# Cross-covariance attention: Grams of two heads over 64 partitions with masked keys, query norms from squares, query casts on GpSimd

## The chip, the core and the metric

The kernel runs on one core of a Trainium2 chip. The metric is device time in microseconds (us) of one execution, smaller is better. The core has a matrix engine (TensorE, PE in the profile; its weight loads are PEld), a vector engine (VectorE, DVE), a scalar engine (ScalarE, ACT), a general engine (GpSimd, POOL) and a sync engine (SyncE, SP), which here only issues DMA transfers. Each engine works through its own queue in order; semaphores hold an instruction back until what it needs is there.

## The reference

Q, K and V have 8 batches, 12 heads, 512 rows and 64 columns (float32). Per head the columns of Q and K are normalised over the rows, a 64x64 matrix of their products is put through a softmax, and V is multiplied by it:

```python
Q_norm = Q / (np.linalg.norm(Q, axis=-2, keepdims=True) + 1e-10)
K_norm = K / (np.linalg.norm(K, axis=-2, keepdims=True) + 1e-10)
attn = np.einsum('bhnd,bhne->bhde', Q_norm, K_norm)
attn = np.exp(attn - np.max(attn, axis=-1, keepdims=True))
attn = attn / (np.sum(attn, axis=-1, keepdims=True) + 1e-10)
return np.einsum('bhnd,bhde->bhne', V, attn).astype(np.float32)
```

Each of the three inputs and the output is 12.58 MB, so 37.75 MB are read and 12.58 MB written.

## The kernel before

**Tiling.** The 96 heads are cut into 24 units `u` of 4 heads (`HU`), two units make a pair `s` (12 pairs), two pairs a group `w` (6 groups). In a unit each head lies on 32 partitions, 16 rows (`T`) of 64 columns on each. Q and K of a pair come into one tile `qk32` of 2 MB (pool of 3), V of half a group into `v32` of 1 MB (pool of 3). Output leaves from tiles `so` of 0.5 MB (pool of 13), two for each pair.

**Stages of a unit or pair**, by the keys that the planner uses:

- `cq` (L212): VectorE casts q and k of a unit to bf16, side by side in `qkb`.
- `gr` (L232): for each row block `t` and each head a matmul of the 32 partitions' [q k] with itself; one head's Gram matrix of 128x128 holds q·q, q·k and k·k. 64 matmuls for a unit; the last unit (`WIDE`) is loaded in another layout and takes 32 over 64 partitions.
- `sq` (L239) and `rd` (L251): VectorE multiplies the diagonal blocks with an identity and sums them, which gives the squared norms of q and k. `kq` (L166 by way of `copy`): the cross block is copied out of PSUM, mostly by ScalarE.
- `pw` (L257, L258): ScalarE takes the power -1/2 as exp(-ln/2). `rq` (L269, L270) copies the q factors to where they are used. `sc` (L262): GpSimd multiplies the cross block with the k factors.
- `lg` (L275): TensorE transposes the result into PSUM. `ex` (L281): ScalarE takes the exponential with its row sum, four instructions for a pair. `nm` (L287, L290): VectorE takes a reciprocal and makes two products, written to `ab` in bf16.
- `cv` (L170 on GpSimd, L168 on VectorE): V is cast to bf16. `vt` (L301): TensorE transposes it; `vc`: the transposes are copied out of PSUM to `vt` by ScalarE, in the last groups also by VectorE.
- `ou` (L318): TensorE multiplies V with `ab`; `oc` copies the result out of PSUM to `so` by ScalarE, for the last 8 heads' pairs also by VectorE; `st` (L206) stores it.

**Order.** Nothing is ordered by the hardware across engines except by semaphores, so the order in each queue is what the program writes. `Order.run` is a planner: each piece has a cost on each engine that may take it (in the table of `piece` calls), the pieces that it needs (`after`), pieces that it has to come behind, and a rank from the table `R`; `BIAS` adds to a cost only when an engine is chosen. The planner goes through time, each time taking the startable piece of the best rank, and the kernel is emitted in the order of the planned starts. Its costs know nothing of two engines that hinder each other. Loads and stores are pieces of an engine "DMA": nearly all of them are issued by SyncE in the planned order, with at most 8 under way (`QUEUE`); each waits for the buffer that it fills or for the data that it stores. `QK_PACE`, `V_FROM`, `V_PACE` and `ST_LAG` are the ranks of loads and stores.

Of the kernel before, what the change touches and what calls it, by code (L numbers as in the profile page):

```python
# [102 lines left out]
def kernel(  # L103
# [14 lines left out]
    WIDE = U - 1  # L118
# [13 lines left out]
    Qw = Q.rearrange("b h (p j) d -> (b h p j d)", j=J).rearrange("(u m p x) -> u p m x", m=2, p=128, x=J * D)  # L132
    Kw = K.rearrange("b h (p j) d -> (b h p j d)", j=J).rearrange("(u m p x) -> u p m x", m=2, p=128, x=J * D)

# [5 lines left out]
    NB = dict(qk=3, v=3, vb=2, qkb=2, vt=2, so=13, sm=2, ab=4)  # L140
# [4 lines left out]
    qkp = ctx.enter_context(tc.tile_pool(name="qkp", bufs=NB["qkb"]))  # L145
    vtp = ctx.enter_context(tc.tile_pool(name="vtp", bufs=NB["vt"]))
# [6 lines left out]
    ps_g = grams_only.enter_context(tc.tile_pool(name="ps_g", bufs=1, space=bass.MemoryType.PSUM))  # L153
# [8 lines left out]
    qk32, v32, vb, qkb, gram, scr, kq, n2, r8, kqs, rq, lg, ex, ab, vps, vt, po, so = ({} for _ in range(18))  # L162
# [9 lines left out]
    def load_qk(s, x, r):  # L172

        w, e = divmod(s, 2)
        if s not in qk32:
            qk32[s] = qp.tile([128, 2, 2, T, D], F32, name="qk32")
        if HELD == ("l" + "qk"[x], s, r):

            nc.vector.memset(qk32[s][0:1, x, r, 0, 0:1], 0.0)
        if (s, x) == (0, 1):  # L180
            nc.scalar.dma_start(out=qk32[s][:, x, r].rearrange("p t d -> p (t d)"), in_=Ku[w, e, :, r])
        elif 2 * s + (r or 0) >= WIDE:
            nc.sync.dma_start(out=qk32[s][:, x, r].rearrange("p (m j) d -> p m (j d)", m=2), in_=(Qw, Kw)[x][U - 1])
        elif r is None:
            nc.sync.dma_start(out=qk32[s][:, x].rearrange("p r t d -> p r (t d)"), in_=(Qu, Ku)[x][w, e])
        else:
            nc.sync.dma_start(out=qk32[s][:, x, r].rearrange("p t d -> p (t d)"), in_=(Qu, Ku)[x][w, e, :, r])
# [20 lines left out]
    def cast_qk(u, x):  # L208
        s, r = divmod(u, 2)
        if x == 0:  # L210
            qkb[u] = qkp.tile([128, T, 2 * D], BF16, name="qkb")
        nc.vector.tensor_copy(qkb[u][:, :, x * D:(x + 1) * D], qk32[s][:, x, r])  # L212
# [7 lines left out]
    def grams(u):  # L220


        s, r = divmod(u, 2)
        if r == 0:
            gram[s] = ps_g.tile([128, HU, 2, 2, 2 * D], F32, name="gram")
        for t in range(T if u < WIDE else J):
            for h in range(HU):
                if u < WIDE:
                    x = qkb[u][32 * h:32 * (h + 1), t, :]
                else:  # L230
                    x = qkb[u][64 * (h % 2):64 * (h % 2 + 1), J * (h // 2) + t, :]
                nc.tensor.matmul(gram[s][:, h, r, 0], x, x, start=(t == 0), stop=(t == (T if u < WIDE else J) - 1))  # L232

    def squares(s, n):

        if n == 0:
            scr[s] = small.tile([128, 2 * HU, D], F32, name="scr")
        half = (LO, HI)[n]
        nc.vector.scalar_tensor_tensor(  # L239
            out=scr[s][half], in0=gram[s][half, :, :, 0, half].rearrange("p h r d -> p (h r) d"), scalar=1e-20,  # L240
            in1=eye2[half, None, :].to_broadcast([D, 2 * HU, D]), op0=ALU.add, op1=ALU.mult,
        )

    def cross(eng, s):

        kq[s] = small.tile([128, 2 * HU, D], F32, name="kq")
        copy(eng, kq[s][HI], gram[s][HI, :, :, 0, LO].rearrange("p h r d -> p (h r) d"))

    def sums(s):
        n2[s] = small.tile([128, 2 * HU], F32, name="n2")  # L250
        nc.vector.tensor_reduce(out=n2[s], in_=scr[s], axis=mybir.AxisListType.X, op=ALU.add)  # L251
# [8 lines left out]
    def scale_k(eng, s):  # L260
        kqs[s] = small.tile([128, 2 * HU, D], F32, name="kqs")
        (nc.vector if eng == "DVE" else nc.gpsimd).tensor_tensor(  # L262
            out=kqs[s][HI], in0=kq[s][HI], in1=r8[s][HI, :, None].to_broadcast([D, 2 * HU, D]), op=ALU.mult,
        )

    def scales_q(s):

        rq[s] = small.tile([128, HU], F32, name="rq")
        nc.scalar.copy(rq[s][LO], r8[s][LO, 0::2])  # L269
        nc.scalar.copy(rq[s][HI], r8[s][LO, 1::2])  # L270

    def logits(s):
        l = lg[s] = ps_l.tile([128, HU, D], F32, name="lg")
        for h in range(HU):
            nc.tensor.transpose(l[:, h, :], kqs[s][HI, 2 * h:2 * h + 2].rearrange("p r d -> p (r d)"), eye2[HI])  # L275

    def exps(s):
        e = small.tile([128, HU, D], F32, name="ex")
        z = small.tile([128, HU], F32, name="esum")
        for h in range(HU):  # L280
            nc.scalar.activation(e[:, h, :], lg[s][:, h, :], AF.Exp, scale=rq[s][:, h:h + 1], accum_out=z[:, h:h + 1])  # L281
        ex[s] = (e, z)
# [45 lines left out]
    for i in range(2):  # L328
        const.tile([128, D // 4], F32, name=f"front{i}")
# [15 lines left out]

    abs_ = []
# [5 lines left out]
    def size(key):  # L352
        if key[0] == "gr" and key[1] >= WIDE:
            return 64
        return 8 if key[0] == "vt" and key[-1] is not None else {"gr": 128, "lg": 8, "vt": 16, "ou": 16}[key[0]]
# [3 lines left out]
    R = dict(cq=2.5, gr=2.471, sq=0.756, kq=1, rd=3.457, pw=3.5, sc=1, rq=1.9, lg=5, ex=1.1, nm=2.545, cv=1.165, vt=0.9, vc=1.1, ou=2, oc=0.9)  # L359
    BIAS = dict(sc=-0.6, kq=5, cv=1, vc=-0.3, oc=0.6)  # L360
    QK_PACE, V_FROM, V_PACE, ST_LAG = 0.631, 0.0377, 0.7486, 1.5133
# [4 lines left out]
    def piece(key, engines, after, behind, rank, fn, *args):  # L366
        if key[0] in ("cv", "vc", "oc", "kq", "sc"):
            plan.add(key, engines, after, behind, rank, lambda eng: fn(eng, *args))
        else:
            plan.add(key, engines, after, behind, rank, lambda eng: fn(*args))  # L370
# [12 lines left out]
    for s in range(S):  # L383
        free = [back("cq", 2 * s + r, 2 * NB["qk"], x) for r in range(2) for x in range(2)]
        for r in parts(s):
            at = QK_PACE * (2 * s + (r or 0)) / U
            for x in range(2):
                key = loaded(x, s, r)
                piece(key, {"DMA": X if r is not None else 2 * X}, free, [last], at, load_qk, s, x, r)
                last = key  # L390
    for u in range(U):
        s, r = divmod(u, 2)
        piece(("cq", u, 0), {"DVE": 0.72}, [loaded(0, s, r), back("gr", u, NB["qkb"])], [back("cq", u, 1, 1)], R["cq"] + 0.01 * u, cast_qk, u, 0)
        piece(("cq", u, 1), {"DVE": 0.72}, [loaded(1, s, r)], [("cq", u, 0)], R["cq"] + 0.01 * u, cast_qk, u, 1)
        piece(("gr", u), {"PE": 1.6}, [("cq", u, 0), ("cq", u, 1), back("kq", s, 1)], [back("gr", u, 1)], R["gr"] + 0.01 * u, grams, u)
    for s in range(S):
        SM = NB["sm"]

        piece(("sq", s, 0), {"DVE": 0.70}, [("gr", 2 * s), ("gr", 2 * s + 1), back("rd", s, SM)], [], R["sq"] + 0.01 * s, squares, s, 0)
        piece(("sq", s, 1), {"DVE": 0.70}, [("gr", 2 * s), ("gr", 2 * s + 1)], [("sq", s, 0)], R["sq"] + 0.01 * s, squares, s, 1)  # L400
        piece(("kq", s), {"ACT": 0.60, "DVE": (0.70, BIAS["kq"])}, [("sq", s, 0), ("sq", s, 1), back("sc", s, SM)], [], R["kq"] + 0.01 * s, cross, s)
        piece(("rd", s), {"DVE": 0.69}, [("sq", s, 0), ("sq", s, 1), back("pw", s, SM)], [], R["rd"] + 0.01 * s, sums, s)
        piece(("pw", s), {"ACT": 0.5}, [("rd", s), back("rq", s, SM), back("sc", s, SM)], [], R["pw"] + 0.01 * s, powers, s)
        piece(("sc", s), {"POOL": (1.04, BIAS["sc"]), "DVE": 1.2}, [("pw", s), ("kq", s), back("lg", s, SM)], [], R["sc"] + 0.01 * s, scale_k, s)
        piece(("rq", s), {"ACT": 0.45}, [("pw", s), back("ex", s, SM)], [], R["rq"] + 0.01 * s, scales_q, s)
        piece(("lg", s), {"PE": 0.6}, [("sc", s), back("ex", s, 1)], [], R["lg"] + 0.01 * s, logits, s)
        piece(("ex", s), {"ACT": 1.30}, [("lg", s), ("rq", s), back("nm", s, NB["sm"])], [], R["ex"] + 0.01 * s, exps, s)
# [6 lines left out]
    for w in range(W):  # L414
# [12 lines left out]
        for n, (q, f) in enumerate(turns(w)):  # L427
# [3 lines left out]
            else:  # L431
                wait = [("kq", S - 1)] + ([("vc", w, *turns(w)[n - 4])] if n >= 4 and turns(w)[n - 4][1] is not None else [])
            piece(("vt", w, q, f), {"PE": 0.6 if f is not None else 0.8}, [("cv", w, r, c) for r in range(2) for c in range(2)] + wait, [turned],
# [7 lines left out]
    for s in range(S):  # L441
        for x in range(4):
# [4 lines left out]
            piece(("ou", s, x), {"PE": 0.5}, [("vc", s // 2, *t) for t in turns(s // 2) if t[0] // 2 == k] + [("nm", s)] + wait, order, R["ou"] + 0.01 * s, outs, s, x)  # L447
# [50 lines left out]
```

## Time and profile before

Median of 3 runs: 128.52 us (128.44 to 128.66). The profiled execution took 128.35 us, of which the profile's span, from the first instruction to the last, is 126.5 us; 1.85 us lie around it.

| engine | busy us | share of the span | instructions |
|---|---|---|---|
| PE (weight loads beside it: 64.2) | 78.9 | 62% | 2128 |
| DVE | 90.7 | 72% | 141 |
| ACT | 72.5 | 57% | 220 |
| POOL | 37.4 | 30% | 40 |
| DMA queue of SyncE (share of 16 engines) | | 96.5% | 15050 packets |

Busy time is the union of an engine's instructions; a wait inside an instruction that has begun counts as busy. The mean duration of a group can be longer than the time that its instruction needs alone, which is how one sees that something held it. The granted TensorE clock was 0.839 of full speed in the mean.

### The profile page before, as it was taken

The numbers are of one execution on the slowest core, as the hardware profiler recorded it, in microseconds if no ns is written. First come the engines' busy times: TensorE is split into PE (matmuls) and PEld (weight loads), VectorE is DVE, ScalarE is ACT, GpSimd is POOL, SyncE is SP. The second block draws the span as 40 slices with busy tenths as digits, with TensorE's granted clock in tenths as the row PEclk, the third lists the DMA queues.
The fourth block names the chain that finished last, engine by engine and source line by source line (L and its number), as shares of the span: only waits on it lengthen the run. The fifth ranks groups of instructions, "written<-read, shape, count | busy, mean of one in ns | idle before, by whom it ended". The sixth has DMA issues, their size and how long they took to land.

```text
span 126.5 us, 4885 instructions
## 1 busy us (share of the span) xinstructions
PE 78.9 (62%) x2128; PEld 64.2 (51%) x2128; DVE 90.7 (72%) x141; ACT 72.5 (57%) x220; POOL 37.4 (30%) x40
## 2 busy tenths in 40 slices
PE   0065393895964679958583999596676858473000
PEld 0054382784843568747372788484464746352000
DVE  3344749839899499899976798999999799740000
ACT  4000441539789077695883688694758969974000
POOL 4006307300745913043064303133363270300000
PEclk9999999999599555899998559959999999855555
DMA  3999999999999999999999999999999999999993
GB/s 129 408 434 411 427 413 421 413 434 408 430 417 418 409 422 417 398 414 425 422 417 412 418 419 421 416 423 423 401 415 411 402 401 407 400 407 408 405 382 149
DMA packets 15359, 50.64 MB, mean 400 GB/s; under 512 B 1130, under 2 KB 1130, under 8 KB 13930
## 3 DMA queue, kind: packets, MB, share of 16 engines
q1 hardware_dynamic: 15050, 49.29, 96.5%
q10 hardware_dynamic: 288, 1.05, 2.1%
q8 instruction: 16, 0.26, 0.7%
q14 instruction: 5, 0.04, 0.1%
HBM read 37.75 MB, written 12.58 MB: 398 GB/s over the span
## 4 chain that ended last, share of the span: by engine, by line
DVE 34%; DMA 21%; PE 19%; ACT 10%; issue 5%; POOL 2%; SPq 0%; DVEq 0%; ACTq 0%; POOLq 0%
DMA qk<-in_Q_dram 21%; DVE qkb L212 12%; PE gram L232 12%; DVE scr L239 7%; DVE ab L290 5%; ACT so L166 4%; PE po L318 3%; DVE vb L168 3%; ACT ex L281 3%; PE vps L301 3%; DVE n L251 3%; DVE vt L168 2%; ACT vt L166 2%; DVE so L168 1%; POOL kqs L262 1%
## 5 line engine op out<-in xcount | busy, mean ns | idle before, releaser
L232 PE MATMUL gram<-qkb 32*128 32x128 bf16 (+1 forms) x1504 | 36.9, 262 | 20.3 <-DVE qkb L212 7.1
L232 PEld LDWEIGHTS <-qkb 32*128 32x128 bf16 (+1 forms) x1504 | 31.0, 117 | 24.8 <-DVE qkb L212 8.9
L212 DVE CAST qkb<-qk 128x1024 bf16<-128x1024 f32 x48 | 35.3, 758 | 8.4 <-DMA qk<-in_Q_dram 6.8
L170 POOL TENSOR_SCALAR vb<-v 128x1024 bf16<-128x1024 f32 x19 | 22.0, 1169 | 43.9 <-DMA v<-in_V_dram 39.6
L166 ACT COPY so<-po 128x512 f32<-128x512 f32 x45 | 24.8, 593 | 6.6 <-PE po L318 6.5
L166 ACT COPY vt<-vps 128x1024 bf16<-128x1024 bf16 (+1 forms) x18 | 17.8, 987 | 16.5 <-PE vps L301 16.4
L318 PE MATMUL po<-ab,vt 128*64 128x128 bf16 x384 | 20.8, 252 | 5.1 <-ACT so L166 1.7
L301 PE MATMUL vps<-identb,vb 128*128 128x128 bf16 x192 | 18.4, 247 | 6.5 <-POOL vb L170 4.3
L262 POOL TENSOR_TENSOR kqs<-kq,r 64x512 f32<-64x512 f32 x12 | 14.1, 1171 | 26.7 <-ACT r L258 14.0
L239 DVE SCALAR_TENSOR_TENSOR scr<-gram,eye 64x512 f32<-64x512 f32 x24 | 16.5, 687 | 6.0 <-PE gram L232 5.8
L318 PEld LDWEIGHTS <-vt 128*64 128x64 bf16 x384 | 15.2, 127 | 9.4 <-issue 4.8
L301 PEld LDWEIGHTS <-vb 128*128 128x128 bf16 x192 | 13.5, 110 | 10.2 <-POOL vb L170 5.5
L281 ACT ACTIVATE ex<-lg,rq 128x64 f32<-128x64 f32 x48 | 14.5, 322 | 2.5 <-PE lg L275 2.3
L166 ACT COPY kq<-gram 64x512 f32<-64x512 f32 x12 | 7.0, 581 | 13.5 <-DVE scr L239 13.3
L290 DVE TENSOR_TENSOR ab<-ex,rinv 64x256 bf16<-64x256 f32 x24 | 13.4, 556 | 0.6
L281 ACT ACTIVATION_READ_ACCUMULATOR ex<-lg,rq 128x1 f32 x48 | 10.2, 213 | 0.0
L275 PE MATMUL lg<-eye,kqs 64*128 64x64 f32 x48 | 6.4, 258 | 4.3 <-POOL kqs L262 2.6
L251 DVE TENSOR_REDUCE n<-scr 128x8 f32<-128x512 f32 x12 | 8.1, 679 | 0.1
L168 DVE COPY vt<-vps 128x1024 bf16<-128x1024 bf16 (+1 forms) x8 | 7.9, 1020 | 0.1
L168 DVE CAST vb<-v 128x1024 bf16<-128x1024 f32 x5 | 7.0, 1399 | 1.3 <-DMA v<-in_V_dram 1.3
L275 PEld LDWEIGHTS lg<-eye,kqs 64*128 64x128 f32 x48 | 4.5, 156 | 6.1 <-POOL kqs L262 3.3
L287 DVE RECIPROCAL rinv<-esum 128x4 f32<-128x4 f32 x12 | 2.1, 172 | 3.4 <-ACT ex L281 3.2
(17 smaller groups left out, 16.0 us busy)
## 6 DMA issues: line engine op xcount, KB each, us to landing
out_dram<-so SPq DMA_DIRECT2D x23, 512.0 KB, 10.2
v<-in_V_dram SPq DMA_DIRECT2D x11, 1024.0 KB, 17.1
qk<-in_Q_dram SPq DMA_DIRECT2D x8, 1024.0 KB, 17.1
qk<-in_K_dram SPq DMA_DIRECT2D x8, 1024.0 KB, 17.9
qk<-in_Q_dram SPq DMA_DIRECT2D x8, 512.0 KB, 12.2
qk<-in_K_dram SPq DMA_DIRECT2D x6, 512.0 KB, 12.5
qk<-in_K_dram ACTq DMA_DIRECT2D x2, 512.0 KB
v<-in_V_dram SPq DMA_DIRECT2D x2, 512.0 KB
```

The lines of the kernel that those rows point to most:

```text
L166: nc.scalar.copy(o, i)
L168: nc.vector.tensor_copy(o, i)
L170: nc.gpsimd.tensor_scalar(out=o, in0=i, scalar1=1.0, scalar2=0.0, op0=ALU.mult, op1=ALU.add)
L212: nc.vector.tensor_copy(qkb[u][:, :, x * D:(x + 1) * D], qk32[s][:, x, r])
L232: nc.tensor.matmul(gram[s][:, h, r, 0], x, x, start=(t == 0), stop=(t == (T if u < WIDE else J) - 1))
L239: nc.vector.scalar_tensor_tensor(out=scr[s][half], in0=gram[s][half, :, :, 0, half].rearrange("p h r d -> p (h r) d"), scalar=1e-20, in1=e ...
L251: nc.vector.tensor_reduce(out=n2[s], in_=scr[s], axis=mybir.AxisListType.X, op=ALU.add)
L262: (nc.vector if eng == "DVE" else nc.gpsimd).tensor_tensor(out=kqs[s][HI], in0=kq[s][HI], in1=r8[s][HI, :, None].to_broadcast([D, 2 * HU, ...
L281: nc.scalar.activation(e[:, h, :], lg[s][:, h, :], AF.Exp, scale=rq[s][:, h:h + 1], accum_out=z[:, h:h + 1])
L290: nc.vector.tensor_tensor(out=a[half, :, half], in0=e[half], in1=ri[half, :, None].to_broadcast([D, HU, D]), op=ALU.mult,)
L301: nc.tensor.transpose(ps[:, c, n, :], vb[w][:, J * c + j].rearrange("p r d -> p (r d)"), identb)
L318: nc.tensor.matmul(po[s, x][e * D:(e + 1) * D, j].rearrange("p r d -> p (r d)"), v, ab[s][:, h, :])
```

## The change

- **Casts.** The cast of q (`cq`, x = 0) may go to GpSimd or VectorE, with a bias of -31.74 for GpSimd; in the program that comes out all 24 are on GpSimd. All 24 casts of V are on GpSimd too (19 before). In `qkb` k now lies first and q second.
- **Masks** (`mk`, new). VectorE writes a tile `km` for each unit by two products of k with a column of `pick` (1 on the partitions of even or odd heads, 0 elsewhere).
- **Grams over 64 partitions.** For each row block two matmuls of 64 partitions instead of four of 32: weights [k of the even head, k of the odd head] with zeros, moving side [k q]. 32 matmuls for every unit. A Gram tile holds k·k and k·q of both heads one above the other; q·q is not in it. `ps_g` has two buffers instead of one.
- **Norms of q** (`q2` and `nq`, new). ScalarE squares q into bf16 (`square_q`), 24 instructions; TensorE sums the squares over partitions with a mask `heads` of 4 columns, 8 matmuls for a unit (`norms_q`). ScalarE copies the sums (`hq`), VectorE adds the two halves (two instructions in `sums`).
- **Smaller pieces.** `squares`: one instruction of 128x256 for a pair instead of two of 64x512; `cross`: 128x256 instead of 64x512, in the program all on VectorE; `scale_k`: 128x256, all on GpSimd; `rq` is gone; `lg`: two transposes instead of four.
- **Order.** New ranks, biases and costs for the planner; the four ranks of loads and stores are 0. In SyncE's queue the first V load comes behind eight units of Q and K instead of behind the first two, and four stores instead of five stand before the last load. The last unit is loaded as the others are (4 KB for each partition's row instead of 2 KB pieces). In the new program VectorE copies 16 output blocks (3 before) and 5 transposed V blocks (8 before).

```diff
-    ps_g = grams_only.enter_context(tc.tile_pool(name="ps_g", bufs=1, space=bass.MemoryType.PSUM))
+    ps_g = grams_only.enter_context(tc.tile_pool(name="ps_g", bufs=2, space=bass.MemoryType.PSUM))
...
-    def cast_qk(u, x):
+    def cast_qk(eng, u, x):
         s, r = divmod(u, 2)
         if x == 0:
-            qkb[u] = qkp.tile([128, T, 2 * D], BF16, name="qkb")
-        nc.vector.tensor_copy(qkb[u][:, :, x * D:(x + 1) * D], qk32[s][:, x, r])
+            qkb[u] = qkp.tile([128, T, 2, D], BF16, name="qkb")
+        copy(eng, qkb[u][:, :, 1 - x], qk32[s][:, x, r])
+
+    def mask_k(u):
+
+        km[u] = kmp.tile([128, T, 2, D], BF16, name="km")
+        for a in range(2):
+            nc.vector.tensor_scalar(
+                out=km[u][:, :, a], in0=qkb[u][:, :, 0], scalar1=pick[:, a:a + 1], scalar2=None, op0=ALU.mult)
+
+    def square_q(u):
+        s, r = divmod(u, 2)
+        q2[u] = q2p.tile([128, T, D], BF16, name="q2")
+        nc.scalar.activation(q2[u], qk32[s][:, 0, r], AF.Square)
...
-            gram[s] = ps_g.tile([128, HU, 2, 2, 2 * D], F32, name="gram")
-        for t in range(T if u < WIDE else J):
-            for h in range(HU):
-                if u < WIDE:
-                    x = qkb[u][32 * h:32 * (h + 1), t, :]
-                else:
-                    x = qkb[u][64 * (h % 2):64 * (h % 2 + 1), J * (h // 2) + t, :]
-                nc.tensor.matmul(gram[s][:, h, r, 0], x, x, start=(t == 0), stop=(t == (T if u < WIDE else J) - 1))
...
+            gram[s] = ps_g.tile([128, 4, 4 * D], F32, name="gram")
+        for t in range(T):
+            for g in range(2):
+                rows = slice(64 * g, 64 * (g + 1))
+                nc.tensor.matmul(
+                    gram[s][:, 2 * g + r, 0:2 * D], km[u][rows, t].rearrange("p a d -> p (a d)"), qkb[u][rows, t].rearrange("p x d -> p (x d)"),
+                    start=(t == 0), stop=(t == T - 1))
+
+    def norms_q(u):
+
+        s, r = divmod(u, 2)
+        for t in range(J):
+            nc.tensor.matmul(
+                gram[s][:, 0, 2 * D + HU * r:2 * D + HU * (r + 1)], q2[u][:, 2 * t:2 * t + 2].rearrange("p t d -> p (t d)"), heads,
+                start=(t == 0), stop=(t == J - 1))
+
+    def squares(s):
+
+        scr[s] = small.tile([128, 4, D], F32, name="scr")
         nc.vector.scalar_tensor_tensor(
...
+            out=scr[s], in0=gram[s][:, :, 0:D], scalar=1e-20,
+            in1=eye2[:, None, :].to_broadcast([128, 4, D]), op0=ALU.add, op1=ALU.mult,
         )
...
-        nc.vector.tensor_reduce(out=n2[s], in_=scr[s], axis=mybir.AxisListType.X, op=ALU.add)
+        nc.vector.tensor_reduce(out=n2[s][:, 0:HU], in_=scr[s], axis=mybir.AxisListType.X, op=ALU.add)
+        for r, (here, there) in enumerate(((LO, HI), (HI, LO))):
+            cols, psum = slice(HU * r, HU * (r + 1)), slice(2 * D + HU * r, 2 * D + HU * (r + 1))
+            nc.vector.scalar_tensor_tensor(
+                out=n2[s][here, HU:2 * HU], in0=gram[s][here, 0, psum], scalar=1e-20, in1=hq[s][there, cols],
+                op0=ALU.add, op1=ALU.add)
...
-    R = dict(cq=2.5, gr=2.471, sq=0.756, kq=1, rd=3.457, pw=3.5, sc=1, rq=1.9, lg=5, ex=1.1, nm=2.545, cv=1.165, vt=0.9, vc=1.1, ou=2, oc=0.9)
-    BIAS = dict(sc=-0.6, kq=5, cv=1, vc=-0.3, oc=0.6)
-    QK_PACE, V_FROM, V_PACE, ST_LAG = 0.631, 0.0377, 0.7486, 1.5133
+    R = dict(cq=1.785, mk=3.054, q2=5.826, gr=4.546, nq=0.886, hq=0.101, sq=0.231, kq=3.274, rd=0.775, pw=0.025, sc=3.251, lg=2.932, ex=-0.237, nm=1.282, cv=1.112, vt=-5.794, vc=3.411, ou=-0.099, oc=0.151)
+    BIAS = dict(cq=-31.74, sc=-60.20, kq=-22.98, cv=64.77, vc=-0.03, oc=0.04)
+    QK_PACE, V_FROM, V_PACE, ST_LAG = 0.0000, 0.0000, 0.0000, 0.0000
...
-        piece(("cq", u, 0), {"DVE": 0.72}, [loaded(0, s, r), back("gr", u, NB["qkb"])], [back("cq", u, 1, 1)], R["cq"] + 0.01 * u, cast_qk, u, 0)
+        piece(("cq", u, 0), {"DVE": 0.72, "POOL": (1.15, BIAS["cq"])}, [loaded(0, s, r), back("gr", u, NB["qkb"])], [back("mk", u, 1)], R["cq"] + 0.01 * u, cast_qk, u, 0)
+        piece(("q2", u), {"ACT": 0.95}, [loaded(0, s, r), back("nq", u, NB["q2"])], [back("q2", u, 1)], R["q2"] + 0.01 * u, square_q, u)
         piece(("cq", u, 1), {"DVE": 0.72}, [loaded(1, s, r)], [("cq", u, 0)], R["cq"] + 0.01 * u, cast_qk, u, 1)
-        piece(("gr", u), {"PE": 1.6}, [("cq", u, 0), ("cq", u, 1), back("kq", s, 1)], [back("gr", u, 1)], R["gr"] + 0.01 * u, grams, u)
+        piece(("mk", u), {"DVE": 0.70}, [("cq", u, 1), back("gr", u, NB["km"])], [("cq", u, 1)], R["mk"] + 0.01 * u, mask_k, u)
+        piece(("gr", u), {"PE": 1.4}, [("mk", u), back("sq", s, 2), back("kq", s, 2), back("rd", s, 2)], [back("gr", u, 1)], R["gr"] + 0.01 * u, grams, u)
+        piece(("nq", u), {"PE": 0.35}, [("q2", u)], [("gr", u), back("nq", u, 1)], R["nq"] + 0.01 * u, norms_q, u)
```

## The prediction

> **What bounds the kernel now.** I read the page's totals and slices first, then the issuing queue's waits, then the end of the timeline, and last the groups and the timeline of VectorE and GpSimd. Totals and slices:
>
> ```profile
> span 126.5 us, 4885 instructions
> PE 78.9 (62%) x2128; PEld 64.2 (51%) x2128; DVE 90.7 (72%) x141; ACT 72.5 (57%) x220; POOL 37.4 (30%) x40
> DVE  3344749839899499899976798999999799740000
> DMA  3999999999999999999999999999999999999993
> SPq L206 <- DMA out_dram<-so: 10.1, 14, 1.0
> ```
>
> The DMA engines are full from the second slice (3.2 us) to the last, at about 410 GB/s: the transfers set the time. The last line, from the waits of SyncE's queue, says that 14 stores waited 10.1 us for earlier transfers, not for data. But VectorE is a close second: between 46 and 112 us its digits are 9 but for a few. So no part of the change can win much, and the question is whether the engines still finish inside the transfers' time. The end of the timeline (start us, us, what) and two 2 us windows show the margin (the last two columns are DMA share and GB/s):
>
> ```profile
> 111.41 0.85 DVE L290 TENSOR_TENSOR ab<-ex,rinv 64x256 bf16<-64x256 f32 x2
> 114.52 1.07 ACT L166 COPY so<-po 128x512 f32<-128x512 f32 x2 [0.24 <-PE po L318]
> 115.81 4.22 SPq L206 DMA_DIRECT2D out_dram<-so  x4
> 122.00:124.00 2.00, 0.00 (x0) 0.00 (x0) 0.00 (x0) 0.00 (x0) 0.00 (x0) 0.50 0.88 342
> 124.00:126.00 2.00, 0.00 (x0) 0.00 (x0) 0.00 (x0) 0.00 (x0) 0.00 (x0) 0.50 0.34 132
> ```
>
> VectorE's last work ends at 112.3, the last output copy 3.3 us later at 115.6, the transfers at 124.7 (0.34 of 2 us after 124), the span at 126.5, 1.8 us later. A store of 0.5 MB needs 1.3 us at 405 GB/s, and a transfer takes 1.4 us from issue to motion (the first load is issued at 0.74 and the engines move from about 2.1 on). So the last copy could end at 124.7 - 1.3 - 1.4 = 122.0 without moving the end: a margin of 6.4 us. Past it each us on VectorE is a us on the kernel.
>
> What can eat it is in these rows: groups (mean ns after the comma), then VectorE's and GpSimd's timelines at 39 us.
>
> ```profile
> L212 DVE CAST qkb<-qk 128x1024 bf16<-128x1024 f32 x48 | 35.3, 758 | 8.4 <-DMA qk<-in_Q_dram 6.8
> L170 POOL TENSOR_SCALAR vb<-v 128x1024 bf16<-128x1024 f32 x19 | 22.0, 1169 | 43.9 <-DMA v<-in_V_dram 39.6
> L168 DVE CAST vb<-v 128x1024 bf16<-128x1024 f32 x5 | 7.0, 1399 | 1.3 <-DMA v<-in_V_dram 1.3
> L212 DVE CAST qkb<-qk x48: 673/693/1536, 5.3 to 99.1; 128x1024 bf16<-128x1024 f32 x48
> L170 POOL TENSOR_SCALAR vb<-v x19: 1042/1048/1541, 10.7 to 101.7; 128x1024 bf16<-128x1024 f32 x19
> 39.17 2.14 DVE L212 CAST qkb<-qk 128x1024 bf16<-128x1024 f32 x2
> 39.23 1.54 POOL L170 TENSOR_SCALAR vb<-v 128x1024 bf16<-128x1024 f32 x1 [3.07 <-DMA v<-in_V_dram]
> ```
>
> A cast takes 0.69 us on VectorE and 1.05 on GpSimd (medians of the fourth and fifth line). Where both run they exclude each other: GpSimd's begins at 39.23 beside VectorE's first cast and takes 1.54, that is 0.5 waiting and 1.04 of work; it ends at 40.77. VectorE's two casts take 2.14 instead of 1.29 and end at 41.31: the second waited until GpSimd had ended. The casts of V on VectorE, made while GpSimd casts too, take 1.40 in the mean. Ops out of PSUM show no such loss (a squares pair takes 1.39 beside GpSimd and without it). The products of L290 do: 0.425 each in a pair of 0.85, 0.556 in the mean.
>
> **The change on VectorE, alone.** Removed: 24 q casts, 24 x 0.69 = -16.6; 5 casts of V, 5 x 0.69 = -3.5. Squares: two of 64x512 at 0.687 become one of 128x256. A reciprocal of 4 elements takes 0.172 and 512 elements 0.687, so 1.01 ns an element, and 256 take 0.43: 12 x 0.43 - 16.5 = -11.3. The cross copy comes from ScalarE: 12 x 0.43 = +5.2. Sums: 12 x (0.43 + two small ones at 0.17) - 8.1 = +1.1. Output copies 3 to 16: 13 x 0.69 = +9.0. V copies: four of 1.22 and one of 0.68 for 8.1 before: -2.5. Masks: 48 products of 128x1024, bf16 to bf16 in SBUF, of which the trace has none. Below, 0.17 (the reciprocal, next to no data); above, 0.69 (as many elements out of float32). The cast is the nearest row, but half of what it reads is spared, so I take the middle, 0.43: +20.6 (8.2 to 33.1). Sum: +2.0. The durations of one engine's instructions add up to 94.7 where their union is 90.7, because a start overlaps the end ahead, 0.03 an instruction; 49 more instructions: -1.4.
>
> **The change in waits of VectorE for GpSimd.** GpSimd had 19 x 1.05 + 12 x 1.04 = 32.4 us of work of its own; now 48 casts, 50.4, and 12 scalings of 256 elements (320 ns for 64 elements in L344, 1.04 for 512, so 0.63), 7.6: 58.0. Over the 104 us in which both work (5 to 109) that is a share of 0.31 before and 0.56 after. A VectorE op that excludes GpSimd meets a running one with that chance and waits half of 1.04. Before, 48 + 5 casts + 24 products: 77 x 0.31 x 0.52 = 12.4; the rows show 48 x 0.065 + 5 x 0.71 + 24 x 0.13 = 9.8, 0.79 of it. After, 24 casts + 48 masks (SBUF to SBUF like the casts, hence counted) + 24 products: 96 x 0.56 x 0.52 x 0.79 = 22.1. So +12.3. Bounds: nothing, if the masks do not exclude GpSimd and a late VectorE meets it less; 27.9 - 9.8 = +18 with the factor at 1.
>
> The Trainium skill, on the page Perfetto Trace Analysis, section Optimizing Scalar/DVE Operations, warns that GpSimd and VectorE share a read port, so that moving work from one to the other might not help. By that rule the move of the q casts is what costs here, and the trace agrees with the 2.14 us above; if the two did not hinder each other at all, the sum would end below the margin, at the transfers' 128.2.
>
> **Beside other work.** ScalarE: -7.0 (cross) - 4.6 (rq) + 24 squares at the 1.01 of a 128x1024 copy = +24.2, hq 12 x 0.19 = +2.3, 13 output copies fewer -7.7, V copies 18 to 20 +2.0: 72.5 to 81.7, with 40 us to spare. GpSimd: about 58 + its own waits, 65 of 126. TensorE: the 32 matmuls over 64 partitions of the last unit took 1.1 us (99.9 to 101.0), as long as the 64 of other units at full clock, so the Grams win nothing; the 192 norm matmuls cost at most what the 192 V transposes do, 18.4; the logits fall by half, -3: 78.9 to 94 at most. It stays under VectorE. The ten small memsets on GpSimd (0.1 to 0.2 each) end before the first load lands at 5.2. **Queue.** A load of 1 MB lands 17.1 us after its issue (median), where 1.4 + 2.6 would do, so an issue may be 13 us late before the engines run dry. A Q/K tile now is free after GpSimd's cast, VectorE's cast and ScalarE's square; I cost that at nothing by this cover, and at one for one beyond it. V loads that stand later and the store moved behind the loads change the order, not the bytes. The last unit's larger pieces and some 1000 fewer instructions to fetch may give 0.1 to 0.2.
>
> **Sum.** VectorE 90.7 + 2.0 - 1.4 + 12.3 = 103.6, 12.9 more. It idled 17.3 us between its first cast (5.3) and its last product (112.3). 8.5 of these lie before 30 us, where it waits for loads, 8.8 after. I keep them: a late VectorE finds more of its data ready, but masks and Grams now also wait for GpSimd, whose queue puts V casts ahead of q casts. Last product 112.3 + 12.9 = 125.2; last copy 128.5; then 0.1 to issue, 1.4, 1.3 and 1.8: span 133.1. With the profiled execution's 1.85 around it, 134.9. Against the margin: 12.9 - 6.4 = 6.5, on 128.35. The median of the runs is 0.17 above that execution, within the measurement. Forecast **134.9**.
>
> **Rivals.** (1) *The transfers hide it*: not slower. The point is 6.4 us more on VectorE, 97.1 in all. Masks near 0.30 (-6.2) or half of the added waits (-6.2) nearly reach it, both together by far. For it: TensorE and ScalarE have room, the second Gram buffer takes a wait away (1.0 us of `kq` in PE's waits), the 8.8 us of late idle time may shrink. Against: two engines that exclude each other get 96 and 60 turns. Time 128.2, some tenths either way. (2) *Masks no faster than casts*, 0.69: 12.5 us more, and the loads begin to wait: 147. Against it: half the bytes. (3) *TensorE at half clock.* It was granted 0.5 in some 40 of the 126 us. At half clock a unit's Gram takes 1.9, a V transposition of 8 took 1.03 and two output blocks 1.06: 24 x 1.9 + 24 x 1.03 + 24 x 1.03 (norms as transposes) + 24 x 1.06 + 4 = 124 us; from 6.7 on that ends at 131, and with 3 us of tail and waits for operands 138 to 140.
>
> **How the numbers follow.** Forecast, 130 to 139: 0.60. Rival 1: 0.18 (faster 0.10, same 0.06, slower 0.02). Rival 2, anything over 142: 0.10. Rival 3: 0.09. A stall of the load queue or another order of waits: 0.03, one of it faster. A measurement of this kernel tells 0.2% apart, 0.26 us. Faster 0.11, same 0.06, slower 0.83. The range takes in rival 3 and the hidden end: 128.1 to 142.0; the forecast's own is 130 to 139.
>
> **What would show it.** Right: VectorE busy 100 us or more, k casts with a mean well over 0.76, masks with many near or over 1 us beside medians near 0.43, GpSimd's casts over 1.17, a last output copy after 122, and stores at the end that wait for copies instead of earlier transfers, with DMA digits under 9 in the last slices. Wrong: VectorE under 97 and DMA at 9 to the end (rival 1); masks at 0.69 alone (rival 2); VectorE idle for TensorE, with PEclk at 5 for most slices (rival 3).

## The result, and the profile after

The changed kernel takes 138.53 us in the median (137.56 to 139.87, 4 runs) against 128.51 us: slower, ratio 1.075 (95% interval 1.069 to 1.082). Its executions scatter by some 2%, those of the kernel before by 0.2%; ratios here and below leave out executions more than 1.5% above the fastest of their kernel, medians do not. The profiled execution took 137.56 us with a span of 135.8. Four parts of its profile answer to those shown of before. The page's totals and slices:

```profile
span 135.8 us, 3876 instructions
PE 84.8 (62%) x1560; PEld 69.9 (51%) x1560; DVE 104.6 (77%) x194; ACT 80.8 (60%) x210; POOL 65.7 (48%) x79
DVE  3387959569579999269799998999979989899300
PEclk9999855555568685698556986998569985699995
DMA  3999999999999999999999999999999999156595
```

VectorE has 104.6 us of busy time instead of 90.7, GpSimd 65.7 instead of 37.4. The DMA digits are 9 until slice 34 (115.4 us), then come 1, 5, 6, 5, 9 and 5: the transfers no longer set the end, they wait for something. Stretches of 4 us (busy time of PE, PEld, DVE, ACT, POOL, then the granted clock, the DMA share and GB/s) show how much is lost:

```profile
76.00:80.00 4.00, 1.87 (x34) 1.35 (x34) 3.96 (x4) 4.00 (x15) 3.83 (x4) 1.00 0.94 336
80.00:84.00 4.00, 3.83 (x64) 3.27 (x66) 3.50 (x11) 1.89 (x6) 0.84 (x2) 0.57 1.00 328
112.00:116.00 4.00, 3.20 (x54) 2.75 (x54) 3.88 (x7) 2.05 (x4) 2.16 (x2) 0.50 0.87 328
116.00:120.00 4.00, 3.61 (x64) 2.80 (x60) 3.13 (x11) 2.58 (x8) 0.74 (x2) 0.74 0.02 8
120.00:124.00 4.00, 3.35 (x61) 2.63 (x55) 3.92 (x8) 4.00 (x14) 0.48 (x1) 1.00 0.97 375
124.00:128.00 4.00, 2.48 (x48) 1.65 (x49) 2.85 (x6) 3.35 (x13) 0.00 (x0) 1.00 0.31 69
```

At 415 GB/s a stretch would move 1.66 MB. The first two fall short by 1.6 us of transfer, the last four by 8.5: together 10, near the 9.3 us by which the span grew. What the transfers waited for stands in the waits of SyncE's queue (total us, times, longest):

```profile
SPq L182 <- DVE qkb L167: 34.5, 8, 7.7
SPq L203 <- DVE so L167: 11.3, 5, 8.3
```

Loads of Q and K waited 34.5 us for casts of k, most of it covered by transfers under way. Stores waited 11.3 us for output copies on VectorE, once for 8.3, from 107.8 to 116.1 us. That store then waited for a copy on ScalarE and was issued at 119.4, the first since 107.4; this is the hole at 116 to 120 us. Both lines name VectorE. For GpSimd's results the other compute engines hardly waited, and no Gram's wait ended with a cast of q; the longest such wait in the list is TensorE's for a scaled cross block:

```profile
PE lg L293 <- POOL kqs L286: 0.8, 1, 0.8
```

Loads of V did wait for GpSimd's casts (10.7 us in four waits), like those of Q and K mostly beside transfers under way. VectorE's groups, with GpSimd's (busy, mean ns | idle before), and then the smallest, middle and largest duration of masks and k casts:

```profile
L169 POOL TENSOR_SCALAR qkb<-qk 128x1024 bf16<-128x1024 f32 x24 | 27.4, 1141 | 29.6 <-PE gram L238 18.7
L215 DVE TENSOR_SCALAR km<-qkb,pick 128x1024 bf16<-128x1024 bf16 x48 | 32.9, 726 | 0.7
L169 POOL TENSOR_SCALAR vb<-v 128x1024 bf16<-128x1024 f32 x24 | 28.3, 1195 | 0.0
L167 DVE CAST qkb<-qk 128x1024 bf16<-128x1024 f32 x24 | 23.0, 959 | 5.0 <-DMA qk<-in_K_dram 4.1
L309 DVE TENSOR_TENSOR ab<-ex,rinv 64x256 bf16<-64x256 f32 x24 | 14.5, 605 | 0.6
```

```profile
L215 DVE TENSOR_SCALAR km<-qkb,pick x48: 469/487/1335, 7.3 to 113.2; 128x1024 bf16<-128x1024 bf16 x48
L167 DVE CAST qkb<-qk x24: 674/695/1557, 5.7 to 110.7; 128x1024 bf16<-128x1024 f32 x24
```

A mask needs 0.49 us and takes 0.73 in the mean; a cast needs 0.69 and takes 0.96 (0.76 before). Where the rest goes is seen at 77 us, in the timelines of VectorE and GpSimd (start, us, what):

```profile
77.80 2.32 DVE L215 TENSOR_SCALAR km<-qkb,pick 128x1024 bf16<-128x1024 bf16 x2
77.18 2.65 POOL L169 TENSOR_SCALAR vb<-v 128x1024 bf16<-128x1024 f32 x2
```

Two masks, 1.0 us of work, take 2.32 beside two casts that take 2.65 instead of 2.1. From 77.18 to 80.12 that is 2.94 us for four instructions that need 3.1 alone: they run one after another.

### The profile page after: what moved, and what is told of

It is laid out like the page before. It is cut to its first block, busy times and chain, and to the rows that moved or that the text cites. A ratio compares the mean times of both kernels' runs of the same rounds, so it can differ in the third digit from the quotient of the medians.

```text
span 135.8 us, 3876 instructions
## 1 busy us (share of the span) xinstructions
PE 84.8 (62%) x1560; PEld 69.9 (51%) x1560; DVE 104.6 (77%) x194; ACT 80.8 (60%) x210; POOL 65.7 (48%) x79
## 4 chain that ended last, share of the span: by engine, by line
DVE 53%; PE 26%; DMA 5%; issue 5%; ACT 4%; DVEq 0%; ACTq 0%
DVE km L215 17%; PE gram L238 16%; DVE qkb L167 10%; DVE ab L309 8%; DMA qk<-in_K_dram 5%; DVE so L167 5%; PE po L337 4%; DVE vt L167 3%; DVE scr L253 3%; PE vps L320 2%; DVE n L270 2%; DVE n L273 2%; PE gram L246 2%; DVE kq L167 2%; ACT so L165 2%
## 5 line engine op out<-in xcount | busy, mean ns | idle before, releaser
L238 PE MATMUL gram<-qkb,km 64*128 64x128 bf16 x768 | 37.3, 271 | 31.9 <-DVE km L215 31.8
L238 PEld LDWEIGHTS <-km 64*128 64x128 bf16 x768 | 31.9, 123 | 35.5 <-DVE km L215 34.5
L169 POOL TENSOR_SCALAR qkb<-qk 128x1024 bf16<-128x1024 f32 x24 | 27.4, 1141 | 29.6 <-PE gram L238 18.7
L221 ACT ACTIVATE q<-qk 128x1024 bf16<-128x1024 f32 x24 | 25.4, 1062 | 15.8 <-PE gram L246 11.8
L215 DVE TENSOR_SCALAR km<-qkb,pick 128x1024 bf16<-128x1024 bf16 x48 | 32.9, 726 | 0.7
L167 DVE CAST qkb<-qk 128x1024 bf16<-128x1024 f32 x24 | 23.0, 959 | 5.0 <-DMA qk<-in_K_dram 4.1
L165 ACT COPY vt<-vps 128x1024 bf16<-128x1024 bf16 (+1 forms) x21 | 19.8, 955 | 3.7 <-PE vps L320 3.5
L286 POOL TENSOR_TENSOR kqs<-kq,r 128x256 f32<-128x256 f32 x12 | 8.8, 735 | 24.4 <-ACT r L282 20.8
L165 ACT COPY so<-po 128x512 f32<-128x512 f32 x32 | 17.9, 591 | 4.0 <-PE po L337 3.9
L300 ACT ACTIVATE ex<-lg,r 128x64 f32<-128x64 f32 x48 | 14.4, 317 | 2.7 <-PE lg L293 2.7
L167 DVE COPY so<-po 128x512 f32<-128x512 f32 x16 | 10.5, 686 | 0.6 <-PE po L337 0.2
L300 ACT ACTIVATION_READ_ACCUMULATOR ex<-lg,r 128x1 f32 x48 | 10.0, 209 | 0.0
## 6 DMA issues: line engine op xcount, KB each, us to landing
v<-in_V_dram SPq DMA_DIRECT2D x11, 1024.0 KB, 13.7
qk<-in_Q_dram SPq DMA_DIRECT2D x8, 1024.0 KB, 11.5
```

The lines of the kernel that those rows point to most:

```text
L165: nc.scalar.copy(o, i)
L167: nc.vector.tensor_copy(o, i)
L169: nc.gpsimd.tensor_scalar(out=o, in0=i, scalar1=1.0, scalar2=0.0, op0=ALU.mult, op1=ALU.add)
L215: nc.vector.tensor_scalar(out=km[u][:, :, a], in0=qkb[u][:, :, 0], scalar1=pick[:, a:a + 1], scalar2=None, op0=ALU.mult)
L221: nc.scalar.activation(q2[u], qk32[s][:, 0, r], AF.Square)
L238: nc.tensor.matmul(gram[s][:, 2 * g + r, 0:2 * D], km[u][rows, t].rearrange("p a d -> p (a d)"), qkb[u][rows, t].rearrange("p x d -> p (x ...
```

## The experiments

Twelve kernels were run. Eleven are the changed kernel with the edits shown; before_aside is the kernel before with one. Five of them (half_gram, no_q, q_dummy, no_v, no_qv) leave work out or use old data and serve for timing alone. The table sets them side by side. "Waits" is VectorE's time beyond 0.69 for a cast, 0.49 for a mask and 0.425 for a softmax product, summed over the instructions that took longer. "Idle" is the time between the start of VectorE's first cast and the end of its last instruction less its busy time (1.1 us of early memsets left out). These, VectorE's busy time, the last output copy and the span are those of the profiled execution, whose own time stands beside the median; for some kernels it lies at the slow or the fast end of their runs.

| kernel | median us (profiled) | ratio to before, 95% | VectorE busy | waits | idle | last copy | span |
|---|---|---|---|---|---|---|---|
| before | 128.5 (128.4) | 1 | 90.7 | 10.2 | 17.3 | 115.6 | 126.5 |
| after | 138.5 (137.6) | 1.069 to 1.082 | 104.6 | 22.5 | 17.8 | 129.6 | 135.8 |
| half_gram | 137.9 (137.6) | 1.066 to 1.077 | 107.7 | 25.8 | 14.6 | 129.6 | 135.8 |
| q_act | 133.6 (133.2) | 1.037 to 1.044 | 94.5 | 12.4 | 23.4 | 125.2 | 131.4 |
| v_act | 138.5 (135.0) | scatters: 135.0 to 139.7 | 92.6 | 10.4 | 27.3 | 127.5 | 133.2 |
| mask_act | 136.7 (136.9) | scatters: 134.4 to 137.1 | 92.8 | 19.8 | 28.8 | 128.9 | 135.1 |
| no_q | 130.4 (131.2) | 1.005 to 1.017 | 96.0 | 14.2 | 19.4 | 123.5 | 129.4 |
| q_dummy | 139.9 (138.7) | 1.082 to 1.092 | 107.0 | 24.9 | 16.5 | 130.7 | 136.9 |
| no_v | 130.4 (129.9) | 1.003 to 1.020 | 96.8 | 14.8 | 17.9 | 121.9 | 128.1 |
| no_qv | 128.9 (128.9) | 1.002 to 1.004 | 89.5 | 7.6 | 18.4 | 115.0 | 127.1 |
| replan | 132.3 (133.8) | 1.020 to 1.033 | 109.3 | 27.5 | 13.2 | 128.5 | 132.0 |
| replan_free | 135.4 (135.7) | 1.035 to 1.052 | 104.1 | 24.4 | 20.5 | 130.4 | 133.9 |
| ranks | 141.3 (142.4) | 1.078 to 1.095 | 102.8 | 23.4 | 28.4 | 137.1 | 140.6 |
| before_aside | 129.0 (128.3) | 1.001 to 1.008 | 101.7 | 21.9 | 11.3 | 120.3 | 126.5 |

### TensorE's clock

The mean granted clock fell from 0.839 to 0.759, and the Grams wait 31.8 us for masks. Was TensorE late, or is it made to wait?

```diff
-        for t in range(T):
+        for t in range(T // 2):
```

> Leaves out half of the rows of each Gram (16 matmuls for a unit instead of 32); all else stays, on every engine. TensorE's busy time falls by some 18 us and the clock is throttled less. Theory (VectorE sets the time): at most 1.5 us faster, 136 to 138.5, VectorE still at 103 to 105. Rival (TensorE at half clock makes VectorE wait): 5 us or more faster, 133 or less, with VectorE's idle time falling by as much.

137.93 us (ratio 1.066 to 1.077 against 1.069 to 1.082). TensorE's busy time fell from 84.8 to 78.7 us, by 6.1 instead of the 18 expected; the Grams alone fell from 37.3 to 23.2 us, and where the rest went was not traced. No time clear of the scatter was gained, and VectorE's busy time was 107.7 us (103 to 105 expected). So the length of the Grams is not what sets the time. The mean clock hardly changed here (0.784 instead of 0.759), so this run alone says little of the clock. Other executions do: the changed kernel took 139.9 us once at 0.835 and 137.6 at 0.759, q_dummy below took 139.9 and 140.0 at 0.89, and replan below took 131.2 to 133.8 at 0.74 to 0.78. A higher granted clock did not make those shorter. Among the four of half_gram the one at 0.90 was the shortest, by 0.8 us, so some tenths may lie in it.

### Taking work away from GpSimd or VectorE, to ScalarE

```diff
-            emit(eng)
+            emit("ACT" if key[0] == "cq" and key[2] == 0 else eng)
```

> The 24 casts of q go from GpSimd to ScalarE at the same places of the same order; nothing else is changed. Theory (exclusion of VectorE and GpSimd takes VectorE past the margin): GpSimd's own work falls from 58 to 33 us, 0.32 of 104 us, so VectorE's waits fall from the measured 22 to 96 x 0.32 x 0.52 x 0.79 = 12.6, its busy time from 104.6 to about 95, under the 97.1 from which the transfers set the end: 128.5 to 132, the upper part if ScalarE (80.8 + 24 x 1.0 = 105) comes late. Masks' mean from 0.73 to about 0.6. Rival (TensorE's clock, granted 0.76): unchanged, 137 or more. Rival (the order of the queues): little change, 135 or more.

```diff
-            emit(eng)
+            emit("ACT" if key[0] == "cv" else eng)
```

> The 24 casts of V go from GpSimd to ScalarE at the same places of the same order; the casts of q stay on GpSimd. Theory: it takes as much work off GpSimd as moving the q casts does, so VectorE's waits fall as much, to about 12.6, busy to about 95, time 128.5 to 132. Rival (what costs is that masks and Grams now wait for q casts in GpSimd's queue): q stays there, so less is won than by moving the q casts, 134 or more. Rivals clock and order: 135 or more.

```diff
-        for a in range(2):
-            nc.vector.tensor_scalar(
-                out=km[u][:, :, a], in0=qkb[u][:, :, 0], scalar1=pick[:, a:a + 1], scalar2=None, op0=ALU.mult)
+        nc.vector.tensor_scalar(
+            out=km[u][:, :, 0], in0=qkb[u][:, :, 0], scalar1=pick[:, 0:1], scalar2=None, op0=ALU.mult)
+        nc.scalar.activation(km[u][:, :, 1], qkb[u][:, :, 0], AF.Copy, scale=pick[:, 1:2])
```

> The second mask product of each unit goes from VectorE to ScalarE (24 activations with a scale for each partition); both casts stay on GpSimd. Theory: VectorE loses 24 x 0.73 = 17.4 us, busy about 87, well under 97.1, ScalarE about 105: 128.3 to 131, and GpSimd's waits fall. It does not tell exclusion from the masks' own work, but both from the clock and the order. Rivals clock and order: 135 or more.

133.57, 138.51 and 136.68 us. VectorE did what the theory said: busy 94.5, 92.6 and 92.8 us, waits of 12.4 and 10.4 us for the first two (12.6 were expected), 19.8 in the third, where both casts stay on GpSimd. The times did not follow: none reached the range of the theory (128.5 to 132, for the third 128.3 to 131), and v_act and mask_act came out where the rivals had theirs (134 and 135 or more). The totals of the page for the first and the third show what changed places:

```profile
PE 82.3 (63%) x1560; PEld 68.4 (52%) x1560; DVE 94.5 (72%) x194; ACT 101.7 (77%) x234; POOL 38.6 (29%) x55
ACT  3387876672469799999899989989589996868900
```

```profile
PE 84.6 (63%) x1560; PEld 70.0 (52%) x1560; DVE 92.8 (69%) x170; ACT 104.8 (78%) x234; POOL 65.7 (49%) x79
ACT  3375978870679859989979999989887999769910
PE gram L238 <- ACT km L216: 17.4, 7, 8.6
```

ScalarE is now at 102 to 105 us, its digits are mostly 8 and 9 from slice 15 on, and VectorE idles 23 to 29 us instead of 17.8. In the last line, from the waits, the Grams wait 17.4 us for the mask that ScalarE now makes. These three do not test the theory cleanly: what VectorE gained was in part lost again to ScalarE, which stands late in the chain too. q_act still won 5 us of the 10. Why v_act won less, and scatters, was not traced.

### Taking work away without putting it elsewhere

So the next kernels leave casts out, and one keeps GpSimd busy while nobody waits for it.

```diff
+    kept = [const.tile([128, T, 2, D], BF16, name=f"kept{i}") for i in range(2)]
...
-            qkb[u] = qkp.tile([128, T, 2, D], BF16, name="qkb")
-        copy(eng, qkb[u][:, :, 1 - x], qk32[s][:, x, r])
+            qkb[u] = kept[u % 2]
+        if x == 1 or u < 2:
+            copy(eng, qkb[u][:, :, 1 - x], qk32[s][:, x, r])
```

> Leaves out the casts of q after the first two units (their bf16 q stays in two kept tiles and is used again), so nothing goes to ScalarE instead. Theory E (VectorE and GpSimd exclude each other): GpSimd's own work 58 to 35 us, VectorE's waits 22 to about 13, busy about 96: 128.5 to 132. Rival D (Grams and masks wait for q casts that stand in GpSimd's in-order queue): the same time, so only q_dummy and no_v tell them apart. Rival O (an order that was planned with costs without these waits): 134 or more.

```diff
+    aside = [const.tile([128, T, D], BF16, name=f"aside{i}") for i in range(2)]
...
-        if x == 1 or u < 2:
-            copy(eng, qkb[u][:, :, 1 - x], qk32[s][:, x, r])
+        copy(eng, qkb[u][:, :, 1 - x] if x == 1 or u < 2 else aside[u % 2], qk32[s][:, x, r])
```

(against the kernel just shown)

> GpSimd does all casts of q as in the changed kernel, but after the first two units into a tile that nobody reads, and the Grams take the kept q of the first two units: GpSimd's work and the exclusion stay, the wait of the Grams for the q casts goes. Theory E: as the changed kernel, 136.5 to 139. Rival D: as no_q, 132 or less. Rival O: in between at most, 134 or more.

```diff
+    keptv = [const.tile([128, 2 * T, 2, D], BF16, name=f"keptv{i}") for i in range(2)]
...
-            vb[w] = vbp.tile([128, 2 * T, 2, D], BF16, name="vb")
-        copy(eng, vb[w][:, c * T:(c + 1) * T, r], v32[w, r][:, c].rearrange("p (t d) -> p t d", d=D))
+            vb[w] = keptv[w % 2]
+        if w < 2:
+            copy(eng, vb[w][:, c * T:(c + 1) * T, r], v32[w, r][:, c].rearrange("p (t d) -> p t d", d=D))
```

> Leaves out the 16 casts of V after the first two groups (the bf16 V of those is used again); q casts stay on GpSimd. GpSimd's own work 58 to 41 us, VectorE's waits 22 to about 16, busy about 98. Theory E: 129 to 133. Rival D: the q casts no longer stand behind V casts, but still wait for VectorE's and TensorE's buffers: 134 or more. Rival O: 135 or more.

130.35, 139.94 and 130.43 us. Totals and DMA slices of the second, then the masks of the first and of the second:

```profile
PE 81.5 (60%) x1560; PEld 67.2 (49%) x1560; DVE 107.0 (78%) x194; ACT 80.4 (59%) x210; POOL 66.8 (49%) x79
DMA  4999999999999999999999999999999994074595
L216 DVE TENSOR_SCALAR km<-kept,pick 128x1024 bf16<-128x1024 bf16 x48 | 27.1, 606 | 0.7
L215 DVE TENSOR_SCALAR km<-kept,pick 128x1024 bf16<-128x1024 bf16 x48 | 33.6, 741 | 0.7
```

This tells the theories apart. With GpSimd's q casts running but awaited by no Gram, the kernel is as slow as the changed one (139.9, a little above the 136.5 to 139 expected) and VectorE waits 24.9 us. Without them it is 8 us faster than the changed kernel. Leaving out 16 V casts, which are no part of the Grams' chain, gains the same 8 us. So it is not the wait for q in GpSimd's queue (rival D), it is GpSimd's work itself, whichever cast it is: VectorE's waits fall to 14.2 and 14.8 us (13 and 16 were expected). Nor is it that GpSimd's other results come late, since hardly anything waited for them in the changed kernel.

Both left out together:

> Leaves out both the casts of q after the first two units and the casts of V after the first two groups: GpSimd's own work falls from 58 to about 18 us, a share of 0.17, VectorE's waits to about 7 us and its busy time to about 89. Theory of exclusion: the transfers set the end, 128.0 to 129. If the order alone were the cause: 129.5 or more, since the order is that of the changed kernel.

```profile
span 127.1 us, 3791 instructions
PE 75.8 (60%) x1560; PEld 62.5 (49%) x1560; DVE 89.5 (70%) x194; ACT 80.2 (63%) x210; POOL 22.7 (18%) x41
DMA  3999999999999999999999999999999999999991
```

128.94 us, VectorE at 89.5 with 7.6 us of waits, and DMA digits at 9 to the end, as expected. The masks, the norms and the new order then fit under the transfers; 0.3% over the kernel before remains (ratio 1.002 to 1.004), whose cause was not sought.

### The order

The planner's table counts 0.72 for a k cast and 0.70 for two masks, about what they need alone (0.69 and 0.97), not what they take.

```diff
-        piece(("cq", u, 1), {"DVE": 0.72}, [loaded(1, s, r)], ...
+        piece(("cq", u, 1), {"DVE": 0.96}, [loaded(1, s, r)], ...
-        piece(("mk", u), {"DVE": 0.70}, ...
+        piece(("mk", u), {"DVE": 1.45}, ...
-        piece(("nm", s), {"DVE": 1.12}, ...
+        piece(("nm", s), {"DVE": 1.38}, ...
```

(and 0.96 for 0.72 where VectorE might cast q)

> The changed kernel with four costs of the planner set to what the profile measured, waits included: casts of k 0.96 for 0.72, the two masks 1.45 for 0.70, the products of the softmax 1.38 for 1.12 (with the reciprocal), and 0.96 for a q cast on VectorE. The work is the same, the planner may order it otherwise and choose engines anew. Rival O: 128.5 to 133, and VectorE's late idle time falls. Theory E: VectorE still has its work and its waits, 135 or more.

```profile
PE 86.5 (66%) x1560; PEld 71.3 (54%) x1560; DVE 109.3 (83%) x194; ACT 80.6 (61%) x210; POOL 65.1 (49%) x79
DMA  4999999999999999999999999999999999934586
```

132.29 us (ratio 1.020 to 1.033). Every engine has the same number of instructions of each kind as in the changed kernel, so it is the order that differs. VectorE's waits even rose, to 27.5 us, but its idle time fell from 17.8 to 13.2. The transfers run dry at the same 115.5 us, and the last output copy comes only 1.2 us sooner (128.5 against 129.6). More of the gain lies behind it: from the last copy to the end 3.6 us pass instead of 6.2, because the last four stores start sooner and are spread over a longer time than in the changed kernel, where they start at 126.9 us:

```profile
124.12 4.73 SPq L203 DMA_DIRECT2D out_dram<-so  x4
```

So about 6 of the 10 us depend on the order of the same work. I had taken order and exclusion for rivals; both matter. That the gain comes from knowing the longer durations, and not from any other order being better by chance, is not shown: no order with costs changed at random was run, and the next two kernels, in other orders too, took 135.4 and 141.3 us.

```diff
-    BIAS = dict(cq=-31.74, sc=-60.20, kq=-22.98, cv=64.77, vc=-0.03, oc=0.04)
+    BIAS = dict(cq=0.0, sc=-0.6, kq=1.0, cv=1.0, vc=-0.03, oc=0.04)
```

(against replan)

> The replanned kernel with small biases in place of the large ones: the planner now leaves 21 of 24 q casts and 22 of 24 V casts on GpSimd, and gives the 12 cross copies and 4 output copies more to ScalarE. VectorE's own work falls by about 12 x 0.42 + 4 x 0.69 = 8 us plus 2 us of waits, but 5 casts come back, 5 x 0.9: about 104 us where the replanned kernel has 109. Exclusion and order together as explanation: 129.5 to 132, not slower than the replanned kernel's 132.3; something else: as that or slower.

135.39 us: slower than with the large biases, though VectorE has 104.1 us instead of 109.3. The expectation failed: its idle time is 20.5 us. Less work in another order gave nothing.

```diff
-    QK_PACE, V_FROM, V_PACE, ST_LAG = 0.0000, 0.0000, 0.0000, 0.0000
+    QK_PACE, V_FROM, V_PACE, ST_LAG = 0.631, 0.0377, 0.7486, 1.5133
```

> The changed kernel with the four ranks of loads and stores as before the change (0.631, 0.0377, 0.7486, 1.5133 for zeros), so that the planner interleaves V loads and stores as it did; costs and work are the changed kernel's. If the order of loads and stores is what the change lost: 133 or less. If the loss lies in the order of the engines' work planned with costs without waits: 136 or more, as VectorE keeps its 104 us and some 17 us of idle time.

```profile
DMA  4999999999999999999999999999999933750086
```

141.32 us, slower still, with 28.4 us of idle time. The old ranks of loads and stores do not bring back what the change lost.

### The exclusion in the kernel before

```diff
+    aside = [const.tile([128, T, D], BF16, name=f"aside{i}") for i in range(2)]
...
         nc.vector.tensor_copy(qkb[u][:, :, x * D:(x + 1) * D], qk32[s][:, x, r])
+        if x == 1:
+            copy("POOL", aside[u % 2], qk32[s][:, 0, r])
```

> The kernel before, with 24 more GpSimd casts of q into a tile that nobody reads, one behind each cast of k; VectorE keeps all its own work. GpSimd's own work rises from 32 to 57 us, a share of 0.55; VectorE's waits from 9.8 to 77 x 0.55 x 0.52 x 0.79 = 17.4, busy from 90.7 to about 98, one us past the 97.1. Theory of exclusion: 128.5 to 131.5, with VectorE's casts well over their 0.76 mean. If the exclusion in the kernel before were nothing: 128.5 and casts at 0.76.

```profile
PE 79.7 (63%) x2128; PEld 65.0 (51%) x2128; DVE 101.7 (80%) x141; ACT 72.3 (57%) x220; POOL 70.7 (56%) x64
L212 DVE CAST qkb<-qk 128x1024 bf16<-128x1024 f32 x48 | 48.5, 1038 | 5.1 <-DMA qk<-in_Q_dram 3.9
```

129.03 us over 10 runs (128.31 to 130.13; ratio 1.001 to 1.008). The casts of VectorE go from 0.76 to 1.04 us in the mean with 24 GpSimd casts more and nothing else changed: the exclusion by itself. The waits came to 21.9 us, more than the 17.4 expected, and the busy time to 101.7 (98 expected). That is past the 97.1 of the prediction, and still the time hardly moved: VectorE's idle time fell to 11.3 us, and the last copy came at 120.3, inside the margin that ends at 122.0.

## Why the prediction was right, point by point

- **What bounds.** Right: the transfers had a margin, and past it VectorE set the time. The last product ended 1.7 us later than forecast (126.9 against 125.2), the last copy 1.1 later (129.6 against 128.5), the span 2.7 later (135.8 against 133.1).
- **VectorE's own work.** The mask was mis-sized a little: 0.43, the middle of the bounds, against a measured 0.49, 48 x 0.06 = 2.9 us. The pieces of 256 elements took 0.42, 0.42 and 0.41 (0.43), the small sums 0.16 (0.17). VectorE has 53 more instructions, not the 49 counted, a slip of 0.1 us in the overlap. The Trainium skill, on the page VectorE: DVE Perf Modes, section Side-by-side: where the cycles go for N=2048 bf16, counts four elements a cycle and about 158 cycles around them; an estimate from that page for 1024 elements is (256 + 158) / 0.96 = 431 ns. The fastest mask here took 469, the middle one 487, so the measurement is 9 to 13% above it.
- **Waits for GpSimd.** 22.1 forecast, 22.5 measured; that they came so near is in part luck, since other orders of nearly the same work had 23.4 (ranks) and 27.5 (replan), and half_gram 25.8. That they are waits for GpSimd's work, and for any of it, is shown by q_dummy, no_q, no_v and no_qv. The estimate (chance of meeting a running op, times half its length, times a factor from the trace of before) also gave 12.6 for 12.4 and 10.4 in q_act and v_act, 13 for 14.2 in no_q, 16 for 14.8 in no_v and 7 for 7.6 in no_qv, but 17.4 for 21.9 in before_aside. The prediction said that the move of the q casts is what costs here. That is half right: the 24 casts would take VectorE 16.6 us (24 x 0.69), and on GpSimd they cost it 8.3 us of waits (22.5 against 14.2 in no_q). The changed kernel with the casts of q on VectorE was not run. The Trainium skill, on the page SBUF — State Buffer, section Who interferes with whom, says that VectorE's casts and tensor_scalar in their two-port modes and GpSimd hold a shared port pair as an exclusive lock, and products with two inputs in SBUF contend with GpSimd's reads; the 2.32 us of two masks beside 2.65 of two GpSimd casts, and 0.605 for a 0.425 product, agree.
- **Busy times.** VectorE 104.6 (103.6 forecast), GpSimd 65.7 (65), ScalarE 80.8 (81.7), TensorE 84.8 (at most 94; 192 norm matmuls took 8.6 us, not 18.4). One sign named beforehand did not show: GpSimd's casts take 1.14 (q) and 1.20 us (V), 1.17 in the mean of all as before, not more; VectorE has the added waits.
- **Idle time kept.** 17.8 us against the 17.3 taken over. That it came out so is luck more than a rule: over the runs it went from 11.3 to 28.8 with the order and with ScalarE's load. Accordingly "VectorE under 97.1, and the transfers set the end" failed as a criterion: 94.5 us gave 133.6 in q_act, 101.7 gave 129.0 in before_aside. The last output copy against 122.0 did better: 115.0 and 120.3 in the two that came near 129, and 121.9 and 123.5 in no_v and no_q at 130.4, against 125.2 and more in those at 132 and above.
- **The tail.** Mis-sized: 4.6 us from the last copy to the end, for one store; measured 6.2. With 6.2 the margin ends at 126.5 - 6.2 = 120.3 instead of 122.0, which fits no_v (121.9, span 1.6 us longer than before) and before_aside (120.3, span as before). The last stores stood close together: four were issued from 126.9 on, the last at 129.6, and four times 1.3 us of transfer do not fit into the 1.4 + 1.3 of one. This is seen in the timelines of ScalarE and SyncE:

```profile
125.73 3.87 ACT L165 COPY so<-po 128x512 f32<-128x512 f32 x7 [0.60 <-PE po L337]
126.86 3.72 SPq L203 DMA_DIRECT2D out_dram<-so  x4
```

- **The queue of loads.** I costed late releases at nothing, with 13 us of cover. The median time of the 1 MB loads from issue to landing fell from 17.1 to 17.9 us to 11.5 to 13.7, so 3 to 6 us of the cover were used in the median; at 76 to 84 us all of it was, and 1.6 us of transfer were lost.
- **What was missed.** The size came from the right sum, but with a cause left out of it: replan shows that the same work on the same engines costs 6 us less in another order, in good part by a shorter tail. The prediction treated the order as given.
- **Rivals.** (1) The transfers hide it: no, but they do once GpSimd's casts are gone. (2) Masks as slow as casts: no, 0.49. (3) TensorE at half clock: the clock did fall, but half_gram and the executions at other clocks show some tenths of a us in it at most.

## What to carry to other kernels

Moving casts from VectorE to GpSimd relieved VectorE by only half here, because it still cast and scaled in SBUF while GpSimd cast: 16.6 us of casts left it, and 8.3 us of waits came back. Before such a move, count both engines' ops that exclude each other in the trace and add the expected waits to VectorE's own time.

A static order is part of the cost: orders of nearly the same work took 132.3, 138.5 and 141.3 us. Planning with durations as measured beside the neighbours gave the best of them, in one try. And when work goes to a third engine that is itself at 80 of 126 us, look at what waits for that engine: here the q casts on ScalarE won half of the loss back, the V casts and masks less.

## What the runs showed of the hardware

A matmul over 64 partitions with 128 weights and 128 columns ran two at a time at full clock, 33 ns each (32 in 1.07 us): two start 3 ns apart, the next two 56 ns after the first. The 32-partition ones ran four at a time, 17 ns each (64 in 1.07 us). Half as many instructions took the same time. In the profiled execution the granted clock was lower, 0.759 against 0.839, although TensorE was busy for the same 62% of the span: in the PEclk line it first falls to 5 in the sixth slice (17 us), where the kernel before kept 9 until 31 us. But it varies from one execution to the next: the four of the changed kernel had 0.758 to 0.835, those of the kernel before in the later experiments 0.760 to 0.865. What decides it was not tried.
